# From the norm to the experts: gain and shift on gathered rows, scores of rows not yet normalized

## The chip, the cores and the metric

The kernel runs on one core of one Trainium2 chip. The metric is the device time in microseconds (us) of one execution, from the first to the last instruction of the core and what lies around them. The engines are named as in the profile: PE is TensorE's matmuls and PEld its weight loads, DVE is VectorE, ACT is ScalarE, POOL is GpSimd, SP is SyncE, whose queue issues the loads of the weights.

## What is computed

A stack of two decoder layers, and one further block, on 256 tokens of 1024 features in float32. The part that matters here is the same in both layers: the residual sum with the mixer's output (retention in layer 0, a sparse attention in layer 1), a layer norm, a router that picks two of sixteen experts for each token, the experts, and a second norm.

```python
def layer_norm(x, g, b):
    mu = xf.mean(-1, keepdims=True)
    var = jnp.square(xf - mu).mean(-1, keepdims=True)
    y = (xf - mu) * lax.rsqrt(var + LN_EPS) * g + b
...
h = layer_norm(ALPHA * h + mix, ln_mix_g[l], ln_mix_b[l])
h = layer_norm(ALPHA * h + moe(h, router_w, router_b, moe_w_gate[l], moe_w_up[l], moe_w_down[l]),
               ln_ffn_g[l], ln_ffn_b[l])
```

The router takes a sigmoid of `h @ router_w`, adds a bias, keeps the best of four groups of four experts by the sum of its two best, and takes the two best of that group. An expert is `(silu(x @ gate) * (x @ up)) @ down`, weighted by the token's normalized score.

## The kernel before, in words

The 256 tokens are two tiles of 128 (t = 0, 1), kept with tokens on partitions in `h`. Products that need full precision are made of three: each operand is split into a high part (rounded by ScalarE) and a low part (the rest, by VectorE), and `mm3` adds high by high, high by low and low by high (L239 to L241).

*The end of the mixer.* The projection back to 1024 features ends in `ends_a`: the last units of weights (1 MB each) are split first, and then all products of tile 0 are issued and after them all of tile 1, 24 products of 512 columns for each tile.

*The passage.* `ln_route` then works tile by tile. `stats(t)` adds the residual and takes mean and variance by halves (L379, L380), and the reciprocal deviation as a power on GpSimd (L436). `norm(t)` subtracts and scales on VectorE (L391). `scores(t)` transposes the normalized rows on TensorE (L398), brings them to SBUF by ScalarE (L403) and VectorE (L400), and multiplies them with the router's weights (L407), which `router` multiplied by the norm's gain beforehand; the shift's part of the scores comes from eight more products (L308) and enters by the identity (L405). A sigmoid on ScalarE gives the scores (L408). `finish` multiplies the rows by the gain and adds the shift (L411), in VectorE for one step of tile 0 and in GpSimd for the rest. `route(t)` is a chain of small VectorE operations on the 16 scores (L325 to L345), a product that ranks each token in its expert (L353), and the one-hot matrix `S` of the experts' slots (L364). `warm` is a product of no use on TensorE (L457): one of 512 columns after tile 1's statistics, and two of 128 in tile 1's routing.

*The experts.* `moe` splits `h` into `hh` and `hl` (L648, L651 on GpSimd for tile 0, L714 on VectorE for tile 1). Pairs of experts are worked on, eight pairs, 64 slots for each expert. `gather` collects the rows of two pairs by products with `S`; the first two of the eight chunks are gathered for the first two pairs from `h` itself in plain precision (L708), the others from `hh` and `hl` (L699), and evicted to `xg` by ScalarE (L723) or VectorE (L721), 512 columns at a time. `half` is a gate or an up product (L797), `down` the product back (L817), and `scatter` adds a pair's result to `h` (L850); for the first pair it is made new from `hh` and `hl` (L846, L847).

*The loads.* Each layer's experts take 96 units of 1 MB. They go through SyncE's queue in order. `FIRST` says in which buffers the first units of a layer land: those of the experts (0, 1, 2, raw), and others that are free by then, among them `wk`, `y`, `Tl`, `hT` and `h` itself (free once the rows are gathered, L770). `ORDER` fixes the order of loading in layer 1. After that the buffers are used in a cycle.

*What sets the order.* Where nothing is written out, a planner lays out each engine's instructions by the program's order and by costs and due times of its own; `issue_after(x)` keeps the instructions in it behind x.

Of the kernel before, what the change touches and what calls it, by code (L numbers as in the profile page):

```python
# [20 lines left out]
EPS = 1e-5  # L21
# [4 lines left out]
OFFSET = 2.0 ** 20  # what tells the tokens of an expert from the others in their ranks  # L26
# [147 lines left out]
# ---------------------------------------------------------------- kernel body  # L174
class Prog:
# [30 lines left out]
    # PSUM tiles of one bank  # L206
# [48 lines left out]
    def ends_a(self, units, pool=()):  # L255
        """the last units of a projection, (outs, src, aT, k0, nk, tile of aT at k0): one token tile after the other;
        pool: what GpSimd's share of the splits comes after"""
# [6 lines left out]
        last = None  # L264
# [18 lines left out]
    def unit_a256(self, outs, src, aT):  # L283
        """tokens on partitions: outs[t] [128, 256] = aT^T . unit (8 k tiles)"""
# [10 lines left out]
    def router(self, l, pool, room, tags, bufs):  # L295
        """the router's weights with the gain of the norm before it, and what its shift adds to the scores"""
# [3 lines left out]
        gb = room.tile([128, 2, 8], F32, tag=tags[1], name="lnp", bufs=bufs)  # L300
# [5 lines left out]
        p = self.pat([128, 16])  # L306
        for k in range(8):
            nc.tensor.matmul(p, gb[:, 1, k:k + 1].to_broadcast([128, 128]), rw[:, k],  # L308
                             start=k == 0, stop=k == 7)
        nc.vector.tensor_copy(brw, p)  # L310
        return grw, brw

    def route(self, t, pool):
        """the experts of token tile t: two of the best of four groups; the lower index first where equal"""
# [11 lines left out]
        # a group's score: the sum of its two best  # L326
# [8 lines left out]
        # how many of its group come before each one  # L335
# [8 lines left out]
        for c in (self.chb, self.ch):  # L344
            V.scalar_tensor_tensor(c[:, t].rearrange("p (g e) -> p g e", g=4),  # L345
                                   grp[:, :, None].to_broadcast([128, 4, 4]), best[:, 1:2], top,
                                   op0=ALU.is_equal, op1=ALU.mult)
        # the rank of each token within its expert, in order: OFFSET + rank where the expert is the token's
# [10 lines left out]
    def onehot(self, qd, t, r, pool):  # L359
        """which token of tile t has which slot of the experts 4 qd to 4 qd + 3 (r: the ranks)"""  # L360
# [3 lines left out]
        self.nc.vector.tensor_tensor(self.S[:, t], slot, r[:, 4 * qd:4 * qd + 4, None].to_broadcast([128, 4, 64]),  # L364
# [3 lines left out]
    def ln_route(self, po, gb, hT, router, pool):  # L368
        """h = LN(alpha h + po), and each token's experts; hT [128, 2, 8, 128] is room"""
        nc, h = self.nc, self.h  # L370
        V, G = nc.vector, nc.gpsimd
        grw, brw = router
        cs = [slice(j * 512, j * 512 + 512) for j in range(2)]

        def stats(t):
            pre = h[:, t]
            st = self.cp.tile([128, 2, 6], F32, tag="ln_st", name="ln_st", bufs=2)
            for j, c in enumerate(cs):
                V.scalar_tensor_tensor(pre[:, c], pre[:, c], ALPHA1, po[j][t], op0=ALU.mult, op1=ALU.add)  # L379
                V.bn_stats(st[:, j], pre[:, c])  # L380
            mv = self.cp.tile([128, 2], F32, tag="ln_mv", name="ln_mv", bufs=2)
            V.bn_aggr(mv, st.rearrange("p a b -> p (a b)"))
            rs = self.cp.tile([128, 1], F32, tag="ln_rs", name="ln_rs", bufs=2)
            self.rstd(rs, mv[:, 1:2])
            if t:
                self.warm(mv[:, 0:1])
            return mv[:, 0:1], rs

        def norm(t, mean, rs):
            for c in cs:  # L390
                V.tensor_scalar(h[:, t, c], h[:, t, c], mean, rs, op0=ALU.subtract, op1=ALU.mult)  # L391

        def scores(t):
            for j in range(2):
                p = self.ptr([128, 4, 128])
                for k in range(4):
                    kk = 4 * j + k
                    nc.tensor.transpose(p[:, k], h[:, t, kk * 128:(kk + 1) * 128], self.ident)  # L398
                if j:
                    V.tensor_copy(hT[:, t, 4:8], p)  # L400
                else:
                    for k in (0, 2):
                        nc.scalar.copy(hT[:, t, k:k + 2], p[:, k:k + 2])  # L403
            plg = self.pat([128, 16])
            nc.tensor.matmul(plg, self.ident, brw, start=True, stop=False)  # L405
            for k in range(8):
                nc.tensor.matmul(plg, hT[:, t, k], grw[:, k], start=False, stop=k == 7)  # L407
            nc.scalar.activation(self.aff[:, t], plg, AF.Sigmoid)  # L408

        def finish(t, c, n, E):  # L410
            return E.tensor_tensor(h[:, t, c], h[:, t, c], gb[:, n, c], op=(ALU.mult, ALU.add)[n])  # L411

        norm(0, *stats(0))
        scores(0)
        last = stats(1)
        with self.tc.issue_after(self.last_eps.ins):
            for c in cs:
                finish(0, c, 0, V)
        norm(1, *last)
        with self.tc.issue_after(self.last_pool.ins):  # L420
            for c in cs:
                finish(0, c, 1, G)
        scores(1)
        self.route(0, pool)
        for c in cs:
            for n in range(2):
                self.last_pool = finish(1, c, n, G)
        self.route(1, pool)

    def rstd(self, out, var):  # L430
        """out = (var + EPS) ** -0.5"""
        n = var.shape[-1]
        v = self.cp.tile([128, 8], F32, tag="rs_v", name="rs_v", bufs=4)
# [4 lines left out]
    def ln_rows(self, i, gb):  # L438
        """gain and shift of norm i on all partitions, [128, 2, 1024]"""
# [4 lines left out]
    def ln_bcast(self, i, gb):  # L444
        """the same without a load: by ones on the tensor engine"""
# [1222 lines left out]
```

## Time and profile before

| | us |
|---|---|
| median of 3 runs (lowest, highest) | 1499.23 (1496.37, 1500.24) |
| span of the profiled execution, first to last instruction | 1498.9 |
| PE busy in it | 1427.4 |
| DVE busy | 776.1 |
| ACT busy | 555.0 |
| POOL busy | 232.8 |

The record gives no time of its own for the profiled execution beside the runs; its span is 0.3 us under their median. The passage of layer 0 lies at about 208 to 250 us of the span, that of layer 1 at about 657 to 700. Times in the rows are microseconds from the span's start. In a timeline a row has start, length, engine, line, operation, output and inputs, the shape, the number of instructions that it merges, and in brackets how long the engine was idle before and what ended that. A float32 product that is not rounded shows as two records. In the windows the granted clock is a share of 2.4 GHz, and the DMA share is that of 16 engines.

### The profile page before, as it was taken

Reading aid. Unit: us, or ns where it says so; the run is one execution under the profiler, and the core shown is the slowest. Engines: PE = TensorE matmul, PEld = TensorE weight load, DVE = VectorE, ACT = ScalarE, POOL = GpSimd, SP = SyncE. Lnnn points to the kernel's source line nnn. Section 1 sums busy time; section 2 is a strip of 40 time slices with the busy share of each in tenths; the row PEclk is TensorE's granted clock in tenths of the full one; section 3 lists DMA queues with packets and bytes.
Section 4 is the critical chain, followed back from the end, with each engine's and each line's share of the span. In section 5 each row is a group of like instructions: output and inputs, shape, how many; then the busy total and the mean of one; then the engine's idle time right before and its main releaser. Section 6 shows DMA issues by size and latency. Waiting matters only on the chain. (4 is left out here: it accounts for less than half of the span.)

```text
span 1498.9 us, 20993 instructions
## 1 busy us (share of the span) xinstructions
PE 1427.4 (95%) x8363; PEld 1016.1 (68%) x8363; DVE 776.1 (52%) x1229; ACT 555.0 (37%) x978; POOL 232.8 (16%) x206
## 2 busy tenths in 40 slices
PE   7999988998998999989998999999999999899997
PEld 6888764443444875564443444997999999699986
DVE  5655563221215456553221215598999775745445
ACT  3434421110112555611110112566878554344442
POOL 2222121000002420021000001002443320211111
PEclk9999998999999999998998999999999999999999
DMA  9845677999984473166999984553765435545550
GB/s 359 330 155 169 257 279 280 375 417 389 414 351 166 160 273 145 57 255 263 362 419 389 414 319 177 198 207 112 265 211 196 156 127 171 194 144 194 187 179 28
DMA packets 64489, 365.16 MB, mean 244 GB/s; under 512 B 7472, under 2 KB 13120, under 8 KB 27648
## 3 DMA queue, kind: packets, MB, share of 16 engines
q1 hardware_dynamic: 60576, 348.75, 62.0%
q0 software_dynamic: 3808, 15.00, 2.8%
q8 instruction: 68, 1.11, 0.3%
q14 instruction: 37, 0.30, 0.1%
HBM read 362.53 MB, written 1.18 MB: 243 GB/s over the span
## 5 line engine op out<-in xcount | busy, mean ns | idle before, releaser
L230 DVE TENSOR_TENSOR wlo<-raw,whi 128x1024 fp32r<-128x1024 f32 x239 | 297.8, 1251 | 230.3 <-ACT whi L228 229.8
L228 ACT CAST whi<-raw 128x1024 fp32r<-128x1024 f32 x254 | 265.0, 1048 | 308.0 <-PE mm L241 129.9
L797 PE MATMUL mm<-raw,xg 128*64 128x512 f32 x744 | 187.2, 618 | 0.0
L241 PE MATMUL mm<-th,wlo 128*128 128x256 f32 x544 | 154.9, 285 | 4.3 <-DVE wlo L230 4.3
L239 PE MATMUL mm<-th,whi 128*128 128x256 f32 x544 | 155.9, 287 | 0.0
L240 PE MATMUL mm<-tl,whi 128*128 128x256 f32 x544 | 154.8, 285 | 0.0
L797 PEld LDWEIGHTS mm<-raw,xg 128*64 128x64 f32 x744 | 56.5, 141 | 93.2 <-issue 88.7
L241 PEld LDWEIGHTS mm<-th,wlo 128*128 128x128 f32 x544 | 104.2, 192 | 5.7 <-DVE wlo L230 4.7
L239 PEld LDWEIGHTS mm<-th,whi 128*128 128x128 f32 x544 | 104.3, 192 | 2.3 <-issue 1.2
L240 PEld LDWEIGHTS mm<-tl,whi 128*128 128x128 f32 x544 | 104.3, 192 | 1.3 <-issue 1.1
L235 DVE TENSOR_TENSOR y<-mm,y 128x512 fp32r<-128x512 f32 x32 | 22.0, 692 | 143.5 <-ACT y L234 142.3
L230 POOL TENSOR_TENSOR wlo<-raw,whi 128x1024 fp32r<-128x1024 f32 x15 | 37.5, 2505 | 305.7 <-ACT whi L228 305.7
L817 PE MATMUL mm<-raw,wk 128*64 128x512 f32 x344 | 80.5, 596 | 0.9 <-ACT wk L810 0.9
L240 PE MATMUL at<-tl,whi 128*128 128x256 f32 x264 | 74.8, 284 | 0.2 <-DVE tl L235 0.2
L239 PE MATMUL at<-th,whi 128*128 128x256 f32 x264 | 74.7, 283 | 0.2 <-ACT th L234 0.2
L241 PE MATMUL at<-th,wlo 128*128 128x256 f32 x264 | 74.7, 283 | 0.0
L234 ACT CAST y<-mm 128x512 fp32r<-128x512 f32 x32 | 18.7, 586 | 121.0 <-PE mm L817 120.8
L817 PEld LDWEIGHTS mm<-raw,wk 128*64 128x64 f32 x344 | 25.7, 137 | 45.7 <-issue 42.7
L850 DVE TENSOR_TENSOR h<-h,at 128x512 f32<-128x512 f32 x48 | 31.7, 685 | 46.4 <-PE at L844 45.0
L241 PE MATMUL mm<-whi,xl 128*128 128x512 f32 x128 | 51.2, 400 | 0.0
L240 PEld LDWEIGHTS at<-tl,whi 128*128 128x128 f32 x264 | 50.7, 192 | 0.7 <-DVE tl L235 0.4
L239 PEld LDWEIGHTS at<-th,whi 128*128 128x128 f32 x264 | 50.6, 192 | 0.7 <-ACT th L234 0.5
(448 smaller groups left out, 3152.9 us busy)
## 6 DMA issues: line engine op xcount, KB each, us to landing
raw<-in_w_moe SPq DMA_DIRECT2D x136, 1024.0 KB, 9.9
raw<-in_w_in SPq DMA_DIRECT2D x37, 1024.0 KB, 4.9
raw<-in_w_ret SPq DMA_DIRECT2D x31, 1024.0 KB, 5.0
wlo<-in_w_moe SPq DMA_DIRECT2D x40, 512.0 KB, 10.0
whi<-in_w_moe SPq DMA_DIRECT2D x40, 512.0 KB, 9.5
raw<-in_w_up SPq DMA_DIRECT2D x16, 1024.0 KB, 4.8
raw<-in_w_dn SPq DMA_DIRECT2D x16, 1024.0 KB, 4.9
hT<-in_w_moe SPq DMA_DIRECT2D x8, 1024.0 KB, 11.3
```

What stands on the lines that cost most here:

```text
L228: self.nc.scalar.copy(hi, src)
L230: (eng or self.nc.vector).tensor_sub(lo, src, hi.bitcast(F32))
L234: self.nc.scalar.copy(hi, src)
L235: self.last = self.nc.vector.tensor_sub(lo, src, hi.bitcast(F32))
L239: mm(out, lh, rh, start=start, stop=False)
L240: mm(out, lh, rl, start=False, stop=False)
L241: return mm(out, ll, rh, start=False, stop=stop)
L797: P.last_gu = nc.tensor.matmul(p[e * 64:(e + 1) * 64], xg[:, k, s0 + e * 64:s0 + e * 64 + 64], r[e][:, k2], start=k == 0, stop=k == 7)
L817: nc.tensor.matmul(pd[j][e * 64:(e + 1) * 64], hT_[:, k, e * 64:(e + 1) * 64], r[e][:, j], start=k == 0, stop=k == 3)
L850: V.tensor_add(h[:, t, c], h[:, t, c], p)
```

## The change

The passage is written anew, as `ends_route`. Tile 1's products are issued one step (three products) after the other, and pieces of tile 0's work stand between them in TensorE's order: transposes after the first and third step, scores after the fifth, and tile 1's first transposes after the seventh. The rows that are transposed and scored are the residual sums, not normalized: the router's weights carry the gain, and `router` takes from them, by eight more products with -0.5 and one more VectorE operation, what the mean would add; the score is then scaled by the reciprocal deviation and the shift's part added in one VectorE operation. The rows are normalized in place by two ScalarE passes for each tile (Identity with scale and bias, 256 and 768 columns). Gain and shift are not applied before the gather, but to the gathered rows, where features lie on partitions, in the evictions to `xg`, which become one per chunk of 256 columns; the first chunks are gathered from `hh` and `hl` like the others. `h` itself gets gain and shift by four VectorE passes of 1024 columns after the first pair's first gather, and `scatter` of the first pair adds to it in one operation instead of two. `h` is no longer a buffer for weights, and `hT`, which now holds the gain rows in both layers, comes last among the first buffers. The product of no use after tile 1's statistics goes.

```diff
-FIRST = ("0 0 0 1 1 2 2 wk 2 raw raw raw y raw raw Tl sp sp sp h sp hT",
-         "0 0 0 1 1 1 hT wk raw raw raw y raw raw w sp sp sp Tl h 2 sp")
-ORDER = ("", "hT raw raw raw 0 0 0 1 1 1 wk y raw raw w sp sp sp Tl")
+FIRST = ("0 0 0 1 1 2 2 wk 2 raw raw raw y raw raw Tl sp sp sp sp hT",
+         "0 0 0 1 1 1 wk raw raw raw y raw raw w sp sp sp Tl 2 sp hT")
+ORDER = ("", "raw raw raw 0 0 0 1 1 1 wk y raw raw w sp sp sp Tl")
...
-    def ends_a(self, units, pool=()):
+    def ends_a(self, units, pool=(), between=None):
...
-            with self.tc.issue_after(last.ins) if last else nullcontext():
-                for outs, aT, k0, nk, o, (h2, l2) in ps:
-                    for k in range(2):
+            if between and t:
+                for work in between[0]:
+                    work()
+            first = last
+            for outs, aT, k0, nk, o, (h2, l2) in ps:
+                for k in range(2):
+                    with self.tc.issue_after((last if between and t else first).ins) if first else nullcontext():
                         last = self.mm3(outs[t], aT[0][:, o + k, s], aT[1][:, o + k, s], h2[:, k], l2[:, k],
                                         k0 + k == 0, k0 + k == nk - 1)
+                    if between and t:
+                        n += 1
+                        for work in between.get(n, ()):
+                            with self.tc.issue_after(last.ins):
+                                last = work() or last
...
+        for k in range(8):
+            nc.tensor.matmul(p[:, 1], self.mhalf[:, 0:1].to_broadcast([128, 128]), grw[:, k],
+                             start=k == 0, stop=k == 7)
+        nc.vector.tensor_copy(brw, p[:, 0])
+        nc.vector.scalar_tensor_tensor(grw, p[:, 1, None, :].to_broadcast([128, 8, 16]), 1.0 / 512, grw,
+                                       op0=ALU.mult, op1=ALU.add)
...
-    def ln_route(self, po, gb, hT, router, pool):
+    def ends_route(self, units, po, hT, router, pool):
...
+        def pre(t, j):
+            if j == 0:
+                sts[t] = self.cp.tile([128, 2, 6], F32, tag="ln_st", name="ln_st", bufs=2)
+            c = cs[j]
+            V.scalar_tensor_tensor(h[:, t, c], h[:, t, c], ALPHA1, po[j][t], op0=ALU.mult, op1=ALU.add)
+            V.bn_stats(sts[t][:, j], h[:, t, c])
...
+        def transposes(t, j):
+            p = self.ptr([128, 4, 128])
+            for k in range(4):
+                kk = 4 * j + k
+                last = nc.tensor.transpose(p[:, k], h[:, t, kk * 128:(kk + 1) * 128], self.ident)
+            for k in (0, 2):
+                A.copy(hT[:, t, 4 * j + k:4 * j + k + 2], p[:, k:k + 2])
+            return last
...
+        def finish(t):
+            mv, rs = norms[t]
+            lg = self.rt[1][:, 208 + 16 * t:224 + 16 * t]
+            V.scalar_tensor_tensor(lg, plgs[t], rs[:, 0:1], brw, op0=ALU.mult, op1=ALU.add)
+            sig = A.activation(self.aff[:, t], lg, AF.Sigmoid)
+            V.scalar_tensor_tensor(rs[:, 1:2], mv[:, 0:1], -1.0, rs[:, 0:1], op0=ALU.mult, op1=ALU.mult)
+            with self.tc.issue_after(sig.ins):
+                for c in (slice(0, 256), slice(256, 1024)):
+                    A.activation(h[:, t, c], h[:, t, c], AF.Identity, bias=rs[:, 1:2], scale=rs[:, 0:1])
...
+        self.ends_a(units, between={0: [first], 1: [lambda: transposes(0, 0)], 3: [lambda: transposes(0, 1)],
+                                    4: [lambda: pre(1, 0)], 5: [lambda: scores(0)], 6: [lambda: finish(0)],
+                                    7: [lambda: transposes(1, 0)]})
+        pre(1, 1)
+        stats(1)
+        transposes(1, 1)
         scores(1)
+        finish(1)
         self.route(0, pool)
-        for c in cs:
-            for n in range(2):
-                self.last_pool = finish(1, c, n, G)
         self.route(1, pool)
...
         for t in range(2):
-            nc.scalar.copy(hh[:, t], h[:, t])
+            for c, after_ in (((slice(0, 256), P.routed), (slice(256, 1024), P.hot)) if t else
+                              ((slice(0, 1024), P.last_eps),)):
+                nc.scalar.copy(hh[:, t, c], h[:, t, c])
+                with tc.issue_after(after_.ins):
+                    V.tensor_sub(hl[:, t, c], h[:, t, c], hh[:, t, c].bitcast(F32))
+        for t in range(2):
             V.tensor_copy(rk[:, t], prk[:, t])
-        with tc.issue_after(P.last_pool.ins):
-            nc.gpsimd.tensor_sub(hl[:, 0], h[:, 0], hh[:, 0].bitcast(F32))
...
+                first = qd == 0 and k2 == 0
+                if first:
+                    p = [P.ptr([128, 256]) for _ in range(2)]
+                    for t in range(2):
+                        for i in range(2):
+                            mm(p[i], i, t)
...
+                    if k2 % 2 if not first else i:
+                        P.evac = V.tensor_scalar(xg[:, k], pi, P.gbp[:, 0, k:k + 1], P.gbp[:, 1, k:k + 1],
+                                                 op0=ALU.mult, op1=ALU.add)
+                    else:
+                        nc.scalar.activation(xg[:, k], pi, AF.Identity, bias=P.gbp[:, 1, k:k + 1],
+                                             scale=P.gbp[:, 0, k:k + 1])
...
-                        V.scalar_tensor_tensor(h[:, t, c], hl[:, t, c].bitcast(F32), ALPHA1, p, op0=ALU.mult, op1=ALU.add)
-                        V.scalar_tensor_tensor(h[:, t, c], hh[:, t, c].bitcast(F32), ALPHA1, h[:, t, c],
-                                               op0=ALU.mult, op1=ALU.add)
+                        V.scalar_tensor_tensor(h[:, t, c], h[:, t, c], ALPHA1, p, op0=ALU.mult, op1=ALU.add)
...
+        with tc.issue_after(P.evac.ins):
+            for n in range(2):
+                for t in range(2):
+                    V.tensor_tensor(h[:, t], h[:, t], P.gb[:, n], op=(ALU.mult, ALU.add)[n])
```

## Rows read from the trace of the kernel before

**Rows 1.** The page, its first part: busy time, share of the span, instructions.

```profile
PE 1427.4 (95%) x8363; PEld 1016.1 (68%) x8363; DVE 776.1 (52%) x1229; ACT 555.0 (37%) x978; POOL 232.8 (16%) x206
```

**Rows 2.** Windows, layer 0: engines (PE, PEld, DVE, ACT, POOL), clock, DMA share, GB/s.

```profile
213.80:234.80 21.00, 11.35 (x69) 9.68 (x67) 19.14 (x50) 3.81 (x9) 11.14 (x9) 0.72 0.75 301
...
255.00:345.00 90.00, 89.33 (x466) 41.08 (x465) 23.21 (x43) 11.23 (x23) 0.00 (x0) 1.00 0.99 400
```

**Rows 3.** Timeline of the passage in layer 0: start, us, engine, line, operation.

```profile
213.37 0.40 PE L241 MATMUL mm<-whi,ol 128*128 128x512 f32 x1
...
217.09 7.83 POOL L411 TENSOR_TENSOR h<-h,gb 128x512 f32<-128x512 f32 x6
...
220.05 1.25 DVE L325 TENSOR_TENSOR rt<-aff,rb 128x16 f32<-128x16 f32 x1
...
221.34 3.62 DVE L329 TENSOR_TENSOR rt<-rt 128x12 f32<-128x12 f32 x3
...
229.07 0.23 DVE L345 SCALAR_TENSOR_TENSOR ch<-rt 128x16 f32<-128x16 f32 x1
...
230.33 0.18 ACT L408 ACTIVATE aff<-at 128x16 f32<-128x16 f32 x1 [9.20 <-PE mm L353]
...
230.70 0.17 DVE L325 TENSOR_TENSOR rt<-aff,rb 128x16 f32<-128x16 f32 x1
...
233.06 0.42 DVE L364 TENSOR_TENSOR S<-com,mm 128x256 fp32r<-128x256 f32 x1
...
234.80 1.98 PE L797 MATMUL mm<-raw,xg 128*64 128x512 f32 x4
```

**Rows 4.** Timeline of the passage in layer 1.

```profile
662.66 0.39 PE L241 MATMUL mm<-whi,ol 128*128 128x512 f32 x1
...
678.11 2.40 POOL L651 TENSOR_TENSOR hl<-h,hh 128x1024 fp32r<-128x1024 f32 x1 [2.65 <-ACT hh L648]
...
678.24 2.30 DVE L333 SCALAR_TENSOR_TENSOR rt<-rt,com 128x4 f32<-128x4 f32 x1
...
683.25 1.98 PE L797 MATMUL mm<-raw,xg 128*64 128x512 f32 x4
```

**Rows 5.** Durations: timelines of both layers, and two lines' groups (ns, min/median/max).

```profile
662.89 1.03 PE L398 MATMUL tr<-com,h 128*128 128x128 f32 x8
...
663.99 1.96 PE L407 MATMUL at<-rt,hT 128*128 128x16 f32 x16
...
213.81 0.69 DVE L379 SCALAR_TENSOR_TENSOR h<-h,mm 128x512 f32<-128x512 f32 x1 [0.78 <-PE mm L241]
...
L648 ACT CAST hh<-h x4: 1037/1042/1061, 220.1 to 677.9; 128x1024 fp32r<-128x1024 f32 x4
...
L811 DVE COPY wk<-tr x16: 418/425/426, 265.3 to 912.1; 128x256 f32<-128x256 f32 x16
...
239.22 0.71 PE L708 MATMUL tr<-S,h 128*128 128x128 f32 x4
...
99.93 1.85 PE L308 MATMUL at<-rw,lnp 128*128 128x16 f32 x16
```

**Rows 6.** SyncE's timeline, the last expert products of layer 0, and TensorE's waits.

```profile
224.95 0.33 SPq L783 DMA_DIRECT2D hT<-in_w_moe  x1
...
239.33 0.33 SPq L783 DMA_DIRECT2D raw<-in_w_moe  x1
...
423.73 2.88 SPq L783 DMA_DIRECT2D raw<-in_w_moe  x3
...
462.44 5.37 PE L817 MATMUL mm<-raw,wk 128*64 128x512 f32 x24
...
PEld mm L797 <- DMA raw<-in_w_moe: 1.3, 4, 0.4
```

**Rows 7.** Windows at the low clock, layers 0 and 1; columns of rows 2.

```profile
223.40:236.60 13.20, 7.04 (x29) 5.05 (x29) 11.31 (x43) 1.38 (x3) 5.68 (x5) 0.50 0.52 196
...
670.40:687.20 16.80, 11.96 (x48) 8.69 (x48) 12.71 (x41) 3.25 (x7) 9.21 (x7) 0.50 0.45 159
```

More of the change, by code (lines that the diff above doesn't have):

```diff
@@ L299, in router @@
         nc.gpsimd.dma_start(rw, self.I["w_rt"])
-        gb = room.tile([128, 2, 8], F32, tag=tags[1], name="lnp", bufs=bufs)
+        self.gbp = gb = pool.tile([128, 2, 8], F32, name="lnp")
         nc.gpsimd.dma_start(gb, self.I["ln_p"][:, 2 * l:2 * l + 2])
@@ L370, in ln_route @@
         nc, h = self.nc, self.h
-        V, G = nc.vector, nc.gpsimd
+        V, A = nc.vector, nc.scalar
         grw, brw = router
         cs = [slice(j * 512, j * 512 + 512) for j in range(2)]
-        def stats(t):
[L376 to L380, printed above, removed]
-            mv = self.cp.tile([128, 2], F32, tag="ln_mv", name="ln_mv", bufs=2)
[L382 to L387, printed above, removed]
@@ L410, in finish @@
[L410 to L422, printed above, removed]
+        sts, norms, plgs = {}, {}, {}
@@ new lines, in transposes @@
+        def transposes(t, j):
[6 more added lines that the diff above has]
+            return last
+        def scores(t):
+            plgs[t] = p = self.pat([128, 16])
+            for k in range(8):
+                last = nc.tensor.matmul(p, hT[:, t, k], grw[:, k], start=k == 0, stop=k == 7)
+            return last
@@ L423, in ln_route, with first @@
+        def first():
+            pre(0, 0)
+            pre(0, 1)
+            stats(0)
+        self.ends_a(units, between={0: [first], 1: [lambda: transposes(0, 0)], 3: [lambda: transposes(0, 1)],
[4 more added lines that the diff above has]
+        transposes(1, 1)
         scores(1)
+        finish(1)
         self.route(0, pool)
-        for c in cs:
-            for n in range(2):
-                self.last_pool = finish(1, c, n, G)
@@ L613, in retention @@
                 P.unit_a(po[j], W[u + 4 * j + kq], (oh, ol), 4 * kq, 16)
-        P.ends_a([(po[j], W[u + 4 * j + 3], (oh, ol), 12, 16, 12) for j in range(2)])
         P.preload(AF.Sigmoid, on[1][:, 0:1])
-        gb = P.ln_rows(ln, hT_pool.tile([128, 2, 1024], F32, tag="hT", name="gb"))
+        P.gb = P.ln_rows(ln, hT_pool.tile([128, 2, 1024], F32, tag="hT", name="gb"))
         hT = hT_pool.tile([128, 2, 8, 128], F32, tag="Th", name="hT")
-        P.ln_route(po, gb, hT, router, rp)
+        P.ends_route([(po[j], W[u + 4 * j + 3], (oh, ol), 12, 16, 12) for j in range(2)], po, hT, router, rp)
 def moe(P, l, ln, out_pool, small, spill_after=SPILL_AFTER):
@@ L700, in mm @@
                                          start=(t == 0 and n == 0), stop=(t == 1 and n == 1))
[L702 to L723 removed]
+                first = qd == 0 and k2 == 0
[5 more added lines that the diff above has]
+                else:
+                    p = P.ptr([128, 2, 256])
+                    for i in range(2):
+                        for t in range(2):
+                            mm(p[:, i], 2 * k2 + i, t)
+                for i in range(2):
+                    k = 2 * k2 + i
+                    pi = p[i] if first else p[:, i]
+                    if k2 % 2 if not first else i:
+                        P.evac = V.tensor_scalar(xg[:, k], pi, P.gbp[:, 0, k:k + 1], P.gbp[:, 1, k:k + 1],
+                                                 op0=ALU.mult, op1=ALU.add)
+                    else:
+                        nc.scalar.activation(xg[:, k], pi, AF.Identity, bias=P.gbp[:, 1, k:k + 1],
+                                             scale=P.gbp[:, 0, k:k + 1])
             return xg, step
@@ L876, in rest @@
                                     nc.tensor.transpose(p[:, n], hk[:, n % 2, n // 2], P.ident)
-                                V.tensor_copy(hkT.rearrange("p k t c -> p (k t) c"), p)
+                                for k2 in range(2):
+                                    k = 2 * kk + k2
+                                    V.tensor_scalar(hkT[:, k2], p[:, 2 * k2:2 * k2 + 2], P.gbp[:, 0, k:k + 1],
+                                                    P.gbp[:, 1, k:k + 1], op0=ALU.mult, op1=ALU.add)
                                 for t in range(2):
@@ L1197, in nsa @@
             P.unit_a(po[j], I["w_no"][2 * j], (oh, ol), 0, 8)
-        P.ends_a([(po[j], I["w_no"][2 * j + 1], (oh, ol), 4, 8, 4) for j in range(2)])
-        P.ln_route(po, gb, hT, router, rp)
+        P.ends_route([(po[j], I["w_no"][2 * j + 1], (oh, ol), 4, 8, 4) for j in range(2)], po, hT, router, rp)
 def dilated(P, pool, qT, kz, v, yh, yl):
```

57 lines of the change are left out of this document (12 added, 45 removed).

## Prediction

> **What bounds the kernel now.** I read the page first: over the whole span TensorE shows work 95% of the time [rows 1], so only what lengthens its own chain can count. A share over the span hides stages, so next come the windows. In the passage of layer 0, 213.8 to 234.8 us, TensorE is busy 11.35 of 21.0 us at a mean clock of 0.72, while VectorE is busy 19.14; in the stretch 255 to 345 inside the experts TensorE is busy 89.33 of 90 at full clock, and the DMA engines 0.99 [rows 2]. The passage is therefore a VectorE chain with TensorE waiting, and the experts behind it run at TensorE's pace with the loads close behind.
>
> The timeline names the chain [rows 3]. The last product of the projection starts at 213.37 and ends at 213.77. The first expert product starts at 234.80: a gap of 21.0 us. The routing of tile 0 starts on VectorE at 220.05. Its first addition, on 16 elements, takes 1.25 us, and three more on 12 or fewer take 3.62 together; the same addition for tile 1 takes 0.17 at 230.70. While these run, GpSimd does its six 512-column passes of gain and shift (7.83 us from 217.09). That routing ends at 229.30, and a VectorE copy that tile 1's scores need stands in its midst. In layer 1 the gap is 663.05 to 683.25, 20.2 us, with the same stretch: a VectorE operation on 4 elements takes 2.30 exactly beside GpSimd's 2.40 [rows 4].
>
> **The change, part by part.** Durations are from the profiled execution, whose span is 1498.9; the record gives no separate time for it. I add 0.3 for what lies around the span, which makes 1499.2, the median of the runs shown.
>
> *Tile 0's scoring amid tile 1's products.* Its eight transposes (1.03), its sixteen matmul records (1.96) and half of tile 1's transposes (0.5) [rows 5] now stand in TensorE's order between tile 1's products. TensorE is full there, so this delays the last product by 3.5: 217.3 in layer 0, 666.55 in layer 1. No stall is added inside, as I read it: scores stand two steps of three products behind the transposes they need, and these a step behind the sums. By itself this placement gains little, since before the same work stood in a gap that VectorE made.
>
> *The chain behind the last product, layer 0.* The residual addition takes 0.69 [rows 5], to 218.0; normalization no longer comes first, so tile 1's last four transposes follow at 218.1 (0.5). The sixteen score records (1.96) end at 220.6, ScalarE's copies beside them. Scaling the score, priced by a small VectorE operation at 0.2, and the sigmoid at 0.18 [rows 3] with gaps between give 221.1. Meanwhile tile 0's routing fits into VectorE's idle 215.2 to 217.3. Tile 1's routing takes from the addition at 230.70 to the end of the one-hot at 233.48 now, 2.8, and 0.2 ahead of it: 224.1, unstretched, because no long GpSimd pass is left. From the one-hot's end to the first expert product it was 1.3 (233.48 to 234.80), and is kept: 225.4 to 225.5. That is 9.3 earlier than 234.80. Layer 1 has the same 8.2 behind 666.55: 674.75 against 683.25 [rows 4], 8.5 earlier.
>
> *What now stands before the first gather.* It needs the high and low parts of both tiles, where before it took the plain state. ScalarE must run the Identity passes of 256 and 768 columns and the two copies after the sigmoid. A row for Identity does not exist; by the ScalarE copy of 1024 columns, 1.04 [rows 5], the whole is about 2.2 and ends near 223.5, inside the routing's 2.8. I cost it at 0, cover gone at 50% longer passes: then 0 to 1.0 a layer. Both ends stay in the range.
>
> *The first gather.* The old plain-precision products of the first two chunks come in groups of 0.72 (one shown [rows 5]; two such groups stand after the first expert product in each layer). They go: 1.4 a layer. The new evictions are two of 256 columns for one of 512: 0.42 each on VectorE by a 256-column copy [rows 5], and VectorE has the low part's 768 columns in front. Between 0 and 1.0 a layer; I take 0.3, since most of it lies beside expert products.
>
> *The router.* Eight more matmuls with a 16-column result are priced by the existing sixteen records, 1.85 [rows 5], on a TensorE that is full at 99.93: plus 1.85 in each layer. Zero is the lower end, if a wait nearby takes it in.
>
> *Gain and shift of the rows* move to VectorE after the first pair's gather: four 1024-column passes, about 5.5 us by the 512-column addition's 0.69 [rows 5], beside expert products where VectorE idles. GpSimd is free. The row of gains in layer 1 loads earlier, into a buffer idle during attention. The first scatter loses four VectorE passes of that length. All cost 0, as TensorE sets the pace there.
>
> *Loads.* The state no longer holds a unit of weights and the buffer of the gain rows comes last, after those passes: one unit less ahead. On SyncE's queue the last early load goes at 224.95 and the next at 239.33, once the first unit is used [rows 6]; this release moves up with the first expert product. The last expert load of layer 0 is issued by 426.61, and the last expert products run to 467.8 [rows 6]. That lead of some 40 us covers a lost unit of 2.6 (1.05 MB at 400 GB/s [rows 2]). Waits for these loads total 1.3 us [rows 6].
>
> *Sum.* Layer 0: -9.3 - 1.4 + 0.3 + 1.85 = -8.55. Layer 1: -8.5 - 1.4 + 0.3 + 1.85 = -7.75. Together -16.3: 1499.2 - 16.3 = 1482.9, so **1483 us**.
>
> *The clock* is taken as no difference: in both layers it is at half (1.2 GHz) for 13.2 and 16.8 us and comes back 1.8 and 3.9 us after the first expert product [rows 7], and I expect about the same behind a shorter gap. If it stays at 2.4 GHz, half of these, 0.9 and 2.0, comes back.
> The Trainium skill, "TensorE: Matmul & The Clock Gate", section "What's actually happening", holds that the half clock is the default and activity lifts it; that speaks against taking away the product of no use behind tile 1's statistics. The trace agrees that a stretch of little work ends at half clock; by that rule the sum would be the second rival's.
>
> **Rivals.**
> *The experts are bound by their loads.* For it: DMA share 0.99 [rows 2]. Against it: the 1.3 us of waits and the 40 us of lead. Then the gain would be the earlier reload less one unit and less the router: 9.3 - 2.6 - 1.85 and 8.5 - 2.6 - 1.85, together 8.9: 1490. Chance 0.08.
> *The clock falls sooner.* The product of no use after tile 1's statistics is removed. If TensorE drops while tile 1 is scored, transposes, scores and the first gather (0.5 + 1.96 + 0.6) take twice as long, 3.1, and in layer 0 the first products another 0.9: together 7.1, so 1490. Chance 0.12.
> *The order is not as written.* The planner decides the place of tile 0's routing. If it stands after tile 1's statistics, 2.1 a layer returns, and ScalarE's passes behind each other's copies bring 1.0: 6.2, 1489. Chance 0.06.
> *The stretch is not GpSimd's doing (slower).* If small VectorE operations are slow for another cause, routing tile 0 takes 9.2 (220.05 to 229.30 [rows 3]) and sits, from 215.2, ahead of tile 1's residual addition on VectorE: 224.4 instead of 217.3. Tile 1's routing then pays the same 7.2 again. The first product comes 14.3 later than 225.5, at 239.8, 5.0 after today's; with the other terms (-1.1 + 1.85) +5.8, and +6.6 in layer 1: 1512. It decides once both routings together stretch by over 8.5. Against it: the same instructions took 0.17 apiece as soon as GpSimd was idle [rows 3]. Chance 0.08.
>
> **How the numbers follow.** The forecast has 0.66: 1483, of its own from 1476 to 1490. Down: full clock (2.9), no delay of evictions (0.6), some of the router covered (up to 3.7). Up: passes of ScalarE (2.0), evictions (1.4), and a planner that lays out every other stage anew, a few us either way. The three gaining rivals lie at 1489 to 1490 and their upper bounds at 1493. So 1475 to 1493, with the slower case left out. A measurement here tells 0.3%, 4.5 us, from no change. Faster by more: the forecast's and most of the three rivals', 0.87; within: their upper ends, 0.06; slower: 0.07, the last rival but for its mildest form.
>
> **What would show it.** In the changed profile: the last projection product 3 to 4 us later than the last of the old, tile 0's routing without any operation over 0.5 us, and the first expert product 8 to 10 us earlier in both layers; no GpSimd pass longer than a power of one column in the passage; a next load within 5 us of the first expert product; waits on expert loads still under 5 us. Wrong would be: stretched VectorE operations with GpSimd idle, TensorE waiting between tile 1's products, a gap from last product to first expert product over 12 us, or a gain at the first product that is gone by the end of the experts.

## The result, and the profile after

| | runs | median us | lowest to highest |
|---|---|---|---|
| before | 6 | 1498.97 | 1496.37 to 1500.73 |
| changed | 6 | 1510.88 | 1504.69 to 1516.57 |

The ratio is 1.0071, 95% interval 1.0043 to 1.0098: the changed kernel is slower by 0.7%, where 1483 us and a range of 1475 to 1493 were forecast. Its profiled execution took 1505.22 us with a span of 1503.2, near the low end of its runs; the profile of before has 1498.9. So the two traces differ by 4.3 us, the medians by 12.

The passage did what was forecast. Timeline of the changed kernel, layer 0 (columns as in [rows 3]; line numbers are those of the changed file):

```profile
216.43 0.18 DVE L341 TENSOR_TENSOR rt<-aff,rb 128x16 f32<-128x16 f32 x1 [0.28 <-ACT aff L426]
216.64 0.33 DVE L345 TENSOR_TENSOR rt<-rt 128x12 f32<-128x12 f32 x3
...
218.13 0.39 PE L241 MATMUL mm<-whi,ol 128*128 128x512 f32 x1
...
222.96 0.17 DVE L341 TENSOR_TENSOR rt<-aff,rb 128x16 f32<-128x16 f32 x1 [0.22 <-ACT aff L426]
223.17 0.32 DVE L345 TENSOR_TENSOR rt<-rt 128x12 f32<-128x12 f32 x3
...
225.38 0.42 DVE L380 TENSOR_TENSOR S<-com,mm 128x256 fp32r<-128x256 f32 x1
...
227.36 1.12 PE L815 MATMUL mm<-raw,xg 128*64 128x512 f32 x2 [0.16 <-ACT xg L740]
...
234.02 0.33 SPq L801 DMA_DIRECT2D raw<-in_w_moe  x1
```

Tile 0's routing stands before the last product, and its first additions take 0.18 and 0.33 us where they took 1.25 and 3.62 [rows 3]. From the last product to the first expert product it is 9.2 us against 21.4, and the first expert product comes 7.44 earlier, though everything ahead came 2.0 later (the router). In layer 1 it is 10.1 against 20.6 [rows 4]:

```profile
675.75 0.40 PE L241 MATMUL mm<-whi,ol 128*128 128x512 f32 x1
...
685.82 1.12 PE L815 MATMUL mm<-raw,xg 128*64 128x512 f32 x2 [0.16 <-ACT xg L740]
```

The gain is gone where the experts end. The start of the product that waits for the next norm's first statistics (a product of no use, the same in both kernels) marks that place; the two timelines, before and then changed:

```profile
471.81 0.59 PE L457 MATMUL at<-ln_st,com 128*128 128x512 f32 x1
```

```profile
476.78 0.59 PE L475 MATMUL at<-ln_st,com 128*128 128x512 f32 x1
```

From the first expert product to here layer 0 takes 476.78 - 227.36 = 249.4 us, and took 471.81 - 234.80 = 237.0: 12.4 more for the same products. Windows of the changed kernel (columns of [rows 2]) show three of the places where time went:

```profile
255.00:345.00 90.00, 86.22 (x429) 38.74 (x426) 22.54 (x41) 12.71 (x26) 0.00 (x0) 1.00 1.02 424
340.00:360.00 20.00, 8.51 (x26) 2.70 (x24) 2.76 (x4) 1.17 (x2) 0.00 (x0) 0.68 0.66 262
...
551.90:558.70 6.80, 6.80 (x24) 5.93 (x24) 1.04 (x3) 2.24 (x3) 0.00 (x0) 0.50 0.00 0
```

The first row is the stretch of [rows 2]: full clock, and little idle time but for the wait that begins at 342.6. The second holds the branch around the rare work on overflowing experts, in the middle of the stage; the third begins within the router's preparation in layer 1, at 1.2 GHz with TensorE shown busy throughout.

**First place: couples pulled apart.** Each expert product uses half of the array's columns; the products of a pair's two experts can run side by side. The changed kernel's timeline in layer 0, second half of the experts:

```profile
415.29 1.93 PE L835 MATMUL mm<-whi,wk 128*64 128x512 f32 x4
417.15 0.93 PE L468 MATMUL at<-lnr,com 96*128 96x128 f32 x6
418.02 1.93 PE L835 MATMUL mm<-wlo,wk 128*64 128x512 f32 x4
...
420.25 1.94 PE L835 MATMUL mm<-hT,wk 128*64 128x512 f32 x8
```

The last row has four products (two records each) as two couples: 1.94 us. The first and third rows have two products each, one expert's and then the other's, with something between: 1.93 us each. A couple apart costs as much as two couples, 0.85 us more, unless a neighbour fills the other half. The planner that writes out the streams had laid out the expert stage anew: of 384 couples in TensorE's stream 28 are apart (the expectation below counts 29), where before there were 20, and they lie in other places. Some of them find a neighbour: in the traces 60 records start with no other expert record within 0.1 us, against 32 before, which makes 15 couples alone against 8. None of this shows as idle time. The Trainium skill, "TensorEngine Tiling (Array Packing)", section "Key Properties", says that different tiles of the array can execute in parallel; these rows agree where the two products follow each other; pulled apart, they ran one after the other.

**Second place: a second wait behind the branch.** Timeline of TensorE there:

```profile
341.27 1.36 PE L862 MATMUL at<-y,ST 128*128 128x512 f32 x3
...
348.91 0.77 PE L862 MATMUL at<-y,ST 128*128 128x512 f32 x1 [6.28 <-PEq L872]
354.75 1.97 PE L815 MATMUL mm<-raw,xg 128*64 128x512 f32 x4 [5.08 <-issue]
```

Before, there is the first wait alone:

```profile
354.98 0.76 PE L844 MATMUL at<-y,ST 128*128 128x512 f32 x1 [6.07 <-PEq L856]
355.67 6.89 PE L797 MATMUL mm<-raw,xg 128*64 128x512 f32 x22
```

The second wait is put down to "issue": nothing that the profile shows is waited for. A unit of weights lands at 354.71, just ahead of the product, but in the changed kernel's second profile (again, below) the product starts at 354.51 and that unit lands behind it, at 354.69. The DMA view of 345 to 357 us, by queues, has three instruction packets of 16 KB:

```profile
q8 instruction: 3, 0.05, 1.8%
```

They start at 346.3, 352.1 and 355.8 and take some 1.1 us each. Both waits end 1.5 us after a packet has come; the third packet comes behind them. Before, packets start at 352.3 and 358.1: the wait ends 1.5 us after the first, and the second finds TensorE at work. **Third place: the router** of layer 1, seen above; **and the clock elsewhere**, to which the last section comes.

### The profile page after: what moved, and what is told of

Read it like the earlier page. It is cut to its first block, busy times and chain, and to the rows that moved or that the text cites. A ratio compares the mean times of both kernels' runs of the same rounds, so it can differ in the third digit from the quotient of the medians.

```text
span 1503.2 us, 21012 instructions
## 1 busy us (share of the span) xinstructions
PE 1436.5 (96%) x8367; PEld 1018.1 (68%) x8367; DVE 765.0 (51%) x1241; ACT 571.3 (38%) x1008; POOL 212.0 (14%) x192
## 5 line engine op out<-in xcount | busy, mean ns | idle before, releaser
L815 PE MATMUL mm<-raw,xg 128*64 128x512 f32 x720 | 183.3, 619 | 5.4 <-issue 5.1
L835 PE MATMUL mm<-raw,wk 128*64 128x512 f32 x384 | 90.2, 596 | 2.3 <-ACT wk L828 2.3
L815 PE MATMUL mm<-whi,xg 128*64 128x512 f32 x120 | 55.4, 596 | 0.0
L815 PE MATMUL mm<-wlo,xg 128*64 128x512 f32 x120 | 54.8, 595 | 0.0
L823 DVE SCALAR_TENSOR_TENSOR wk<-wk,wsl,mm 128x512 f32<-128x512 f32 x16 | 12.0, 748 | 81.7 <-PE mm L815 81.4
## 6 DMA issues: line engine op xcount, KB each, us to landing
whi<-in_w_moe SPq DMA_DIRECT2D x40, 512.0 KB, 10.1
```

What stands on the lines that cost most here:

```text
L815: P.last_gu = nc.tensor.matmul(p[e * 64:(e + 1) * 64], xg[:, k, s0 + e * 64:s0 + e * 64 + 64], r[e][:, k2], start=k == 0, stop=k == 7)
L835: nc.tensor.matmul(pd[j][e * 64:(e + 1) * 64], hT_[:, k, e * 64:(e + 1) * 64], r[e][:, j], start=k == 0, stop=k == 3)
```

## Experiments

Ratios are against the kernel before, run beside each group: its medians there were 1502.39, 1502.47 and 1501.57 us. "Stage" is the stretch from the first expert product to the mark above, each from one profile.

| run | median us | ratio, 95% interval | stage, layer 0 | layer 1 |
|---|---|---|---|---|
| changed, once more (again) | 1512.98 | 1.0081, 1.0051 to 1.0110 | 247.7 | 239.7 |
| couples kept (pairs) | 1495.24 | 0.9959, 0.9944 to 0.9973 | 242.3 | 235.4 |
| couples kept in before (bpairs) | 1504.29 | 1.0030, 1.0007 to 1.0052 | 235.1 | 240.4 |
| and 8 narrow products (bnarrow) | 1508.50 | 1.0035, 1.0007 to 1.0062 | 234.6 | 241.6 |
| pairs, stream moved (pairs_shift) | 1488.82 | 0.9900, 0.9872 to 0.9928 | 236.2 | 234.3 |
| pairs, router as one product (pairs_router) | 1489.83 | 0.9920, 0.9896 to 0.9945 | 236.8 | 241.4 |
| that, stream moved (shift4) | 1489.77 | 0.9915, 0.9897 to 0.9934 | 236.3 | 237.1 |
| shift4 without interleaving (late) | 1485.27 | 0.9878, 0.9852 to 0.9904 | 237.5 | 234.1 |
| shift4, wide products in attention (shiftwarm) | 1477.86 | 0.9852, 0.9829 to 0.9876 | 236.2 | 233.9 |
| that, two units less ahead (less) | 1483.55 | 0.9870, 0.9841 to 0.9900 | 240.7 | 235.5 |
| bpairs, wide products in attention (bwarm) | 1497.83 | 0.9975, 0.9962 to 0.9987 | 235.0 | 238.0 |

**Couples kept.** The second product of a couple is queued behind the first and at high priority, and the half that lands last goes first (the same in the down projection):

```diff
-                    for e in range(2):
-                        P.last_gu = nc.tensor.matmul(p[e * 64:(e + 1) * 64], ...
+                    first = None
+                    for e in (1, 0):
+                        with ExitStack() as keep:
+                            if first:
+                                keep.enter_context(tc.issue_after(first.ins))
+                                keep.enter_context(tc.high_priority())
+                            first = P.last_gu = nc.tensor.matmul(...
```

> The changed kernel, with one edit: the products of the two experts of a pair (halves of the array, side by side) are kept next to each other in TensorE's stream; in the changed kernel 29 such couples are pulled apart by other products, in the kernel before 20, and a couple apart takes about twice its 0.85 us. Theory order (the gain of the passage is lost in the expert stage because its products were written out in another order): the stretch from the first expert product to the last norm's product of layer 0, 249 us in the changed kernel against 237 before, falls by 7 to 10 us, layer 1's by 2 to 4, the time by 9 to 13 us against the changed kernel, to 1498 to 1502. Theory loads (the expert stage is as long as its weights need to arrive): both stretches stay within 1.5 us, the time stays at 1508 to 1513.

> The kernel before, with the same edit alone (20 couples apart become 6). Theory order: its own couples cost it too, so it gains 3 to 7 us, to 1492 to 1496, less than the changed kernel does by the same edit. Theory loads: within 1.5 us of the kernel before.

On the changed kernel the stages fall by 7.1 and 4.1 us, as the theory of the order has it; loads are not the limit. In the trace 2 couples are left alone, 13 fewer, and 13 times 0.85 is 11.1. The time falls from 1.0071 to 0.9959 of before, 1.1% or 17 us, more than expected. The two profiles differ by 8.3 only, since the clock fell in that of pairs at the start of layer 1's attention; against the changed kernel's second profile, where it fell there too, it is 15.0: 9.7 in the stages, and the rest mostly clock that pairs kept at 2.4 GHz in the block behind the experts. On the kernel before the stages fall by 1.9 and 1.6, but the time grew by 0.3%, against the expectation. In its trace the 4 couples alone in layer 0 are gone (3.4 us, of which some 1.5 go to a longer half clock at the stage's start); those of layer 1 are not. Its profile has the clock at 1.2 GHz for 17.1 us at the start of layer 1's attention, where the kernel before kept it at 2.4; that alone is 7.6 us, by the same instructions on both sides of it.

**The second wait.** Four narrow products of no use, where TensorE is idle, move what follows in the stream. In pairs_shift they stand in layer 0, in shift4 in layer 1:

```diff
         scores(1)
+        for _ in range(extra):
+            self.warm(norms[1][1][:, 0:1], 128)
         finish(1)
```

> As the run with couples kept, and four narrow products of no use (128 columns) in layer 0's passage, where TensorE has nothing to do: TensorE's instructions behind layer 0's branch then lie at another place of the pieces of 16 KB in which they are fetched. Theory fetch (the second wait behind the branch, 5.57 us in that run and 5.08 in the changed kernel, is for the next piece of instructions, because the jump lands on the last few of a piece): that wait goes, the first one of some 6.2 us stays, and the time falls by 4.5 to 6 us against the run with couples kept. Theory loads (that wait is for the unit that landed last): the wait stays, the time within 1 us.

> As the run with couples kept and one product in the router's preparation, and four narrow products of no use in layer 1's passage. In that run layer 0 has one wait behind its branch and layer 1 two (6.28 and 5.45 us). Theory fetch: layer 1's second wait goes, layer 0 keeps one, and the time falls by 4.5 to 6 us against that run; this is then the changed kernel without the three side effects found. Theory loads: no change over 1 us.

TensorE's timeline behind the branch of layer 0 in pairs and then in pairs_shift:

```profile
347.55 0.76 PE L873 MATMUL at<-y,ST 128*128 128x512 f32 x1 [6.10 <-PEq L883]
353.36 5.39 PE L820 MATMUL mm<-raw,xg 128*64 128x512 f32 x12 [5.04 <-issue]
```

```profile
350.40 0.77 PE L875 MATMUL at<-y,ST 128*128 128x512 f32 x1 [6.10 <-PEq L885]
351.10 7.21 PE L822 MATMUL mm<-raw,xg 128*64 128x512 f32 x24
```

The second wait is gone, and the stage is 6.1 us shorter. The second packet comes as late as in pairs (5.7 us behind the first, there 5.8), but TensorE now has products to run until then. The time falls by 0.6% of before, some 9 us, more than expected; the two profiles differ by 4.5. In shift4 the same happens in layer 1 (796.27 and 801.99 in pairs_router; 795.79 and 796.49 here). The time of shift4 did not fall for all that: 4.2 us of gain stand at 806 us in its profile, and clock at 1.2 GHz behind the experts and in the next block takes most of it back. So the wait is for instructions and not for a load, and what it is worth is seen in the stage. The Trainium skill, "Runtime: NRT & Kernel Launch", section "Instruction fetch mechanics", says that a taken branch to a target that was not prefetched forces a fetch of that page, in blocks of 16 KiB; the first wait, in every run here, agrees. The second fits a target near the end of a block, with little to run before the next one comes; where the target lies no run shows.

**The router.** In pairs_router eight products of 16 columns become one of 128 and a reduction on VectorE; in bnarrow the kernel before gets eight more of them.

```diff
-        for k in range(8):
-            nc.tensor.matmul(p[:, 1], self.mhalf[:, 0:1].to_broadcast([128, 128]), grw[:, k], ...
+        nc.tensor.matmul(p[:, 16:144], self.mhalf[:, 0:1].to_broadcast([128, 128]), self.rt[0][:, 0:128], ...
+        nc.vector.tensor_reduce(tot, p[:, 16:144].rearrange("p (k n) -> p n k", k=8), axis=AX.X, op=ALU.add)
```

> As the run with couples kept, and the 8 new narrow products of the router's preparation (16 columns each) become one of 128 columns with a reduction on VectorE behind it. Theory router (8 more narrow products behind 8 others cost 2.4 us in layer 1 and let the granted clock fall to 0.50 for the 6.8 us that follow, 5.2 us in all against 1.85 of the sum; 2.0 us in layer 0): layer 1's queries keep a clock of 1.00 and the time falls by 5 to 7 us against the run with couples kept. Rival (the clock fell there by chance of the moment and not from these products): it falls by 2 to 4 us, and the clock of that place differs from run to run with or without them.

> The kernel before with couples kept, and 8 narrow products of 16 columns added behind the router's own in each layer, their result overwritten. Theory router: 1.9 to 2.4 us a layer, and in layer 1 a granted clock of 0.50 behind them, 3.4 us more: 5 to 8 us slower than the kernel before with couples kept. Rival (chance of the moment): 3.5 to 5 us slower, clock 1.00 there.

The changed kernel's timeline has the old and the new narrow products of layer 1 one behind the other; the clock falls at 551.9, within the second, and the window at 0.50 shown above begins there:

```profile
548.88 1.85 PE L319 MATMUL at<-rw,lnp 128*128 128x16 f32 x16
550.58 2.41 PE L322 MATMUL at<-rt,mhalf 128*128 128x16 f32 x16
```

Windows of bnarrow from the end of its own, in layers 0 and 1, and then of pairs_router over the same work in layer 1:

```profile
102.90:109.70 6.80, 6.80 (x28) 6.39 (x28) 2.10 (x5) 1.04 (x1) 0.39 (x1) 0.50 0.11 48
546.60:553.40 6.80, 6.80 (x25) 6.03 (x25) 0.58 (x3) 2.24 (x3) 0.00 (x0) 0.50 0.00 0
```

```profile
539.00:546.40 7.40, 7.40 (x38) 6.18 (x37) 3.30 (x6) 3.20 (x4) 0.00 (x0) 1.00 0.36 113
```

In the five profiles with the extra narrow products the clock fell behind them in 8 of 10 places; in the eight profiles without them in none of 16. That is hardly chance. Against pairs, pairs_router gains 3.1 us in each layer there (instructions of the same kind compared in time). Its median is 5.4 lower, as expected; that sum hides that layer 0's second wait went and one came in layer 1, since the streams had moved. bnarrow lies 4.7 us behind bpairs after layer 0's router, what the theory gives a layer in which the clock falls. Its median is only 4.2 higher, which is the rival's figure, but the rival's condition, a clock of 1.00 there, does not hold: bpairs lost clock in other places.

**The interleaving alone.** The first tile's steps are called behind the second tile's products instead of among them.

```diff
-        self.ends_a(units, between={0: [first], 1: [lambda: transposes(0, 0)], ...
+        self.ends_a(units)
+        first()
+        transposes(0, 0)
+        ...
```

> As the run before this one, but the first tile's transposes, scores and scaling come behind the second tile's products and not among them: the interleaving alone taken back. By the prediction's sum the interleaving is what takes the first tile's part out of the chain behind the last product: 3 to 5 us a layer from the last product of the projection to the first expert product come back, 6 to 10 us in all. Rival (the gain is the gathering from rows without gain and shift, and the interleaving is worth little): under 3 us in all.

The first expert products of shift4 stand at 225.90 and 676.17, those of late at 226.46 and 676.64. Less what the two differ by ahead of the passages, taking the interleaving back costs 0.6 and 1.0 us. The rival holds. The stretch from the last product to the first expert product grows by 3.8 and 3.2, as the other theory has it, but the last product comes 3.1 and 2.2 earlier. That late's median is 4.5 us lower goes with the clock again (63 us at 1.2 GHz in its profile, 86 in that of shift4).

**The clock at the start of attention.** Wide products of no use, two for each token tile, among the first scores of layer 1, on shift4 and on bpairs:

```diff
                 V.tensor_reduce(nm[:, pr, 0], pc[:, pr], axis=AX.X, op=ALU.max, negate=True)
+                if g == 0:
+                    P.warm(nm[:, pr, 0, 0:1])
```

> As the second run of this call, and four products of 512 columns of no use among layer 1's first attention scores (0.85 us each, 3.4 in all), where the granted clock fell to 0.50 for 17.1 us in the two runs with couples kept that were built on the changed kernel and did not fall in the kernel before. If the clock falls there for want of work, the fall goes and the time changes by -6 to -3 us; if it falls by the moment alone, the time grows by 2 to 4 us or stays within what chance gives.

> The kernel before with couples kept and the four wide products of no use among layer 1's first attention scores, that is with the same side effects taken away as in the best version, whose passages alone then differ from it. Theory of the prediction (the passages give 9.3 and 8.5 us, less the router's preparation): 1490 to 1498, 12 to 20 us over the best version. Rival (what the best version gains comes from the side edits and not from the change): 1478 to 1484.

Windows of shift4 and then of shiftwarm over that start:

```profile
549.40:566.40 17.00, 16.92 (x47) 8.20 (x47) 8.01 (x24) 8.94 (x42) 2.03 (x4) 0.50 0.98 392
```

```profile
546.00:567.00 21.00, 21.00 (x95) 10.47 (x94) 13.91 (x43) 13.44 (x66) 3.69 (x5) 1.00 0.86 350
```

In all three profiles with these products the clock stays at 2.4 GHz; in eight of the ten others it falls there. shiftwarm takes 11.9 us less than shift4, more than expected, and is the best kernel here: 1.5% under before. Of the 14.1 us between the two profiles 5.0 arise at that start, which is what was expected of it; most of the rest is clock in other places, which the edit does not explain. bwarm is the same for the other side: both kernels then have nearly all their couples kept (7 and 2 apart), one wait behind each branch and this stretch at full clock, and they differ by the change with its cheaper router: 1497.83 against 1477.86, 20 us, or 18.5 by their ratios to before. In the profiles 7.1 and 8.2 us of this arise in the two passages, and 4.1 in layer 1's experts, where the 7 couples of bwarm lie. So most of what the forecast added up is there; the rival, that the side edits alone make the gain, falls.

**Loads.** Two places of 1 MB are left out of the list of first places in layer 0 (`Tl` and `y`).

> The best version so far (couples kept, one product in the router's preparation, four narrow products behind the scores, wide ones among the first attention scores), with two weight units of 1 MB fewer loaded ahead of layer 0's expert stage (two buffers left out of the list of first places). Prediction's assumption (the loads run far enough ahead that a unit less costs nothing): layer 0's stretch from the first expert product to the last norm's product within 1.5 us, apart from up to 2.5 us for 6 couples that this order pulls apart. Theory loads (the stage is as long as its weights need to arrive): 4 to 6 us longer, as each unit takes 2.5 us at 420 GB/s.

From 233 to 370 us every landmark lies 0.7 us behind shiftwarm, unchanged: two units less cost nothing there. Behind 370 us the stream is another one (6 couples apart) and 3.7 more come. The stage's 4.6 us lie in the interval of the loads' theory, but TensorE's weight loads wait for expert units as little as before in that part, 1.0 us against 0.8, so late units are not the cause. One more couple runs alone, and TensorE's idle time grows from 1.4 to 3.4 us, with waits for VectorE and ScalarE; the rest is not attributed.

**The changed kernel once more.**

> The changed kernel itself once more, beside the others. All theories: 0.4 to 1.0 percent slower than the kernel before. What the clock does: if it falls behind the router's 16 narrow products because of them, it falls in layer 1 again (near 552 us), and perhaps in layer 0 (near 103 us); if by the moment alone, in neither or elsewhere.

Slower by 0.8%, as expected. The clock fell again behind layer 1's router, from 552.0, and not in layer 0; and this time also at the start of attention, for 13.7 us, which makes 6.1 of the 6.7 us between the two profiles of this kernel.

## Why the prediction was wrong

The step that failed is the one that has no term in the sum: behind the first expert product the stage is taken to last as long as before ("the experts behind it run at TensorE's pace", "All cost 0, as TensorE sets the pace there"). TensorE does set the pace, but its pace was changed, in layer 0: 7.1 us by couples apart, of which the kernel before pays some 3.4 too, and 6.1 by the second wait. That is about 10 of the 12.4 us by which the stage grew, against 9.4 gained in the passage; the other 2 are not attributed. Both come from the streams written out anew, which the prediction named in its range as "a few us either way". It should have asked what in the stage depends on the order of the stream.

Point by point:
- **Chain behind the last product: right in layer 0 partly by luck, too short in layer 1.** Forecast 225.5, with the router's 1.85 later 227.35; measured 227.36. But the last product was delayed by less than forecast, and from its end to the first expert product it is 8.8 where 8.2 were worked out: tile 1's scores wait for its reciprocal deviation on GpSimd, which has no term in the sum. In layer 1 it is 9.7 for the 8.2: ScalarE's copy of tile 0's rows stands ahead of tile 1's sigmoid, and VectorE's low part of tile 0 ahead of its routing, work that the sum put at 0. Timelines, layer 0 and then layer 1:

```profile
220.95 1.46 POOL L454 TENSOR_TENSOR rt<-rs_v,mhalf 128x1 f32<-128x1 f32 x1 [8.65 <-DVE rs_v L452]
222.45 0.23 DVE L425 SCALAR_TENSOR_TENSOR rt<-at,rt 128x16 f32<-128x16 f32 x1 [0.44 <-POOL rt L454]
...
679.20 1.05 ACT L667 CAST hh<-h 128x1024 fp32r<-128x1024 f32 x1 [0.94 <-PE at L419]
680.15 0.21 ACT L426 ACTIVATE aff<-rt 128x16 f32<-128x16 f32 x1
680.28 1.23 DVE L669 TENSOR_TENSOR hl<-h,hh 128x1024 fp32r<-128x1024 f32 x1 [0.76 <-ACT hh L667]
```

- **GpSimd as the cause of the stretch: right.** With GpSimd idle the same operations take 0.17 to 0.33; no run changes GpSimd's work alone. The slower rival's mechanism did not occur, though its time, 1512, is near the result.
- **Delay of the last product, 3.5:** 2.7 and 2.9 against the kernel before, less the router; 3.1 and 2.2 by the run without interleaving. That the placement gains little by itself: right, 0.6 and 1.0 us.
- **Router, 1.85 a layer: right in itself, mis-sized in layer 1 by the clock.** 2.0 in layer 0; 5.2 in layer 1, of which 3.4 are 6.8 us at half clock.
- **Loads: right in the main.** TensorE's weight loads wait for expert units 2.3 us in layer 0, where they waited 1.6 (the prediction's 1.3, and 0.3 for the down products), in pieces of 0.3 to 0.4, and DMA idles behind the branch. The next load came 6.7 us behind the first expert product, not within 5.
- **Clock "no difference": wrong on both sides.** The passages now cost 6.8 us each at half clock instead of 13.2 and 16.8 [rows 7], a gain; the router, the longer wait at the branch and the block behind the experts took it back. The rival of a clock that falls sooner did not come: tile 1 was scored by 221.5 and 679.1, and the clock fell at 224.2 and 681.6. The sign by which this was to be seen, "a gain at the first product that is gone by the end of the experts", is what came.

Of the 12 us between the medians the two profiles carry 4.3: +2.0 by layer 0's router, -9.4 in its passage, +12.4 in its experts, +5.2 by layer 1's router, -7.6 from there to its first expert product, -2.5 in its experts, +4.4 behind, nearly all of it clock. The rest lies in runs at a lower mean clock (0.965 to 0.977, 1516.57 to 1504.69); that the attention's start makes up most of it is read from the second profile and not shown for each run.

## What to carry to other kernels

If a planner writes out the streams, a local change rewrites distant stages: compare the streams of those stages before the times, and pin what the hardware needs adjacent. A busy engine at full clock can still run at half its rate, so compare stretches of equal work and not busy shares. To judge a change of one percent on such a kernel, take away the side effects on both sides and then compare.

## What the runs showed of the hardware

- Over thirty-two records of 16 columns in a row (548.88 to 552.99) the clock fell to 0.50, at 551.9 and for 6.8 us, although TensorE was shown busy 3.00 of 3.00 us in 548.8 to 551.8.
- Behind the branch TensorE waited 6.0 to 6.4 us in each layer of every run, until 1.5 to 1.7 us after a 16 KB packet of instructions had come. The next packet starts 5.5 to 6.0 us behind that one. In 4 of 26 places TensorE had nothing left to run until then and waited 4.9 to 5.1 us more, again until 1.6 us after the packet. Four narrow products ahead in the stream took that second wait away.
- The same instructions kept or lost the clock in different kernels. In the block behind the experts the changed kernel fell to 0.50 twice for 3.4 us, in both its profiles at the same instructions:

```profile
1019.50:1022.90 3.40, 3.40 (x14) 2.31 (x13) 3.40 (x7) 0.59 (x1) 0.00 (x0) 0.50 0.75 237
1104.80:1108.20 3.40, 2.78 (x13) 2.78 (x14) 3.40 (x7) 0.00 (x0) 0.00 (x0) 0.50 0.49 145
```

and the kernel before, over the same work, did not:

```profile
1016.20:1022.00 5.80, 5.70 (x38) 4.28 (x40) 5.80 (x12) 1.11 (x2) 0.00 (x0) 1.00 0.69 219
1101.20:1106.00 4.80, 4.23 (x35) 4.23 (x36) 4.80 (x9) 1.05 (x1) 0.00 (x0) 1.00 0.65 218
```

What decides it in a given kernel was not found.
